# Six of ten gate and value projections of a hybrid decoder block go from seven half-size products to plain products, and the rest are spread one half-step to two other jobs

## The chip, the core and the metric

The kernel runs on one core of a Trainium2 chip. TensorE (PE) multiplies matrices into PSUM, VectorE (DVE) and ScalarE (ACT) work elementwise, GpSimd (POOL) and SyncE (SP) issue DMAs here. The metric is the device time of one execution in microseconds.

## The reference

One layer on 256 tokens of width 2048, all in float32. `h` is the normalised input; one wide projection of it feeds four branches, each is gated, projected back and merged through sigmoid gates that are projections of `h` too; then an output projection, a residual and a last norm.

```python
h = rmsnorm(x, norm_g)
proj = jnp.einsum('bsd,df->bsf', h, w_in)            # 2048 -> 18432, split in 14 pieces
ya = stick_breaking_attention(a_q, a_k, a_v) * jax.nn.silu(a_g)
yb = conformer_conv(b_a, b_b, ...) * jax.nn.silu(b_g)
yc = spatial_gating(jax.nn.gelu(c_u), jax.nn.gelu(c_v), ...) * jax.nn.silu(c_g)
yd = dilated_mixture(d_q, d_k, d_v) * jax.nn.silu(d_g)
yproj = jnp.einsum('bsnc,ncd->bsnd', branches, w_branch)
gates = jax.nn.sigmoid(jnp.einsum('bsd,df->bsf', h, w_gate) + b_gate)
merged = jnp.sum(gates * yproj, axis=2)
return x + jnp.einsum('bsd,de->bse', merged, w_out)  # then rmsnorm(x, final_g)
```

## The kernel before

Every weight is read once or twice from HBM as a tile of 128 x 2048 (1 MB) and split into a high part `hi` (a rounded copy, ScalarE, line 87) and a low part `lo` (the difference, VectorE, line 88). Three products, high by high, low by high and high by low, give nearly float32 precision. `xhl` holds the two parts of the normalised input, `xuh` and `xul` those of the input before the division by its norm.

The work is a list `prog` of jobs. `run` walks it: at position t it issues the loads of job t+5, the split of job t+2, the addition of job t+4, then the matmuls of job t, what follows them (`post`), and whatever `later` has put at this position. Each engine takes its instructions in that order. Kinds of job:

- T (`proj_t`, lines 254 and 257): one weight tile as the stationary side, 16 matmuls of 512 columns and 16 of 256 into one bank of the pool `ps_t`; ScalarE and VectorE empty it (lines 286, 287). 120 of them.
- N (`mm_n`, lines 307 to 309): a weight tile as the moving side, 24 matmuls of 512 columns into a pair of banks. Two make a block of 512 columns of a branch's projection, four one of the other projections.
- H (`group`, line 429): a group of 256 x 2048 by 2048 x 1024 is done by seven products of half-size blocks instead of eight (Strassen's scheme in Winograd's form). Each product is two halves H of 12 matmuls. Factors of the weights are sums of tiles, made in place by `do_add` (line 120, VectorE), those of the input are made once by `make_sx`; the products are combined out of PSUM (lines 408 and 412). A group is 14 H. A gate group adds its bias by one matmul with a constant.

There are ten groups: two for each of the four branches' gates, and the values `a_v` and `c_v`. They stand in a `queue`, from which `step` mixes them in among T and N. Eight N of the values `d_v` come first, on `xuh` and `xul`, scaled afterwards, while the normalisation runs on VectorE. Then follow the convolution's projections, the dilated attention's heads (`d_head`; the convolution's taps and norm on VectorE beside them), the b gates, branch d, the attention pairs (`a_pair`), branches b and a, the c units and branch c, and the output projection. Loaded tiles turn in a ring of six (`st`); gates and values go to DRAM and come back (`gl`, `v`).

## Time and profile before

| what | value |
|---|---|
| time, median of 2 runs (range) | 1641.81 us (1639.13 to 1644.49) |
| the profiled execution: own time, span | 1643.87 us, 1642.2 us |
| TensorE matmuls busy | 1475.0 us, 90% |
| VectorE busy | 1262.8 us, 77% |
| ScalarE busy | 862.5 us, 53% |
| mean granted clock of TensorE | 0.963 |
| DMA | 391.87 MB, mean 239 GB/s |

A busy line gives an engine's time in instructions; PEld is the loading of stationary operands, which overlaps the matmuls. In the view by windows each row is a stretch of the span in microseconds: its length, each engine's busy time with the number of instructions, TensorE's granted clock as a share of full speed, the share of the time that the DMA engines move data, and their rate. In the view by groups a row is a line of the kernel, engine and operation: count, busy time, mean length in ns, and the idle time ahead of them with what ended it. In the view of waits a row is who waited for whom: time in total, number, longest.

### The profile page before, as it was taken

The page shows a single profiled execution, that of the slowest core. Times are in us where ns is not written, and L with a number is a line of the kernel's source. Part 1 is how long each engine was busy: PE and PEld are TensorE (multiplying, and loading weights), DVE is VectorE, ACT ScalarE, POOL GpSimd, SP SyncE. Part 2 cuts the span into 40 slices and gives each one's busy share as a digit, 9 for nine tenths or more (in the row PEclk, how much of TensorE's full clock was granted, in tenths as well). Part 3 has the DMA queues.
Part 4 walks back from the last instruction along what each step waited for, and adds up shares of the span by engine and source line. Part 5 has one row for each costly group of instructions (what it writes and reads, how often), then busy time and mean ns, then how long its engine had stood idle before and what let it go on. Part 6 is the DMA issues. An engine that isn't in the chain of part 4 may idle for free. (4 is left out here: it accounts for less than half of the span.)

```text
span 1642.2 us, 18166 instructions
## 1 busy us (share of the span) xinstructions
PE 1475.0 (90%) x7204; PEld 1227.0 (75%) x7204; DVE 1262.8 (77%) x1232; ACT 862.5 (53%) x773; POOL 86.9 (5%) x160
## 2 busy tenths in 40 slices
PE   7889999999966979999997989878989979978997
PEld 6778888888855767777786877766867768856786
DVE  7588888888778878988776766768778587897654
ACT  6344444444445555754566575656544367755342
POOL 0100000000000000011000000000111200001000
PEclk9999999999998989999999999998999999999999
DMA  8555545554417758799874845756988766869551
GB/s 340 206 186 180 186 173 193 180 181 169 163 52 260 287 200 320 264 336 346 280 276 173 316 176 209 258 215 230 348 307 336 316 246 228 316 249 396 192 205 52
DMA packets 65861, 391.87 MB, mean 239 GB/s; under 512 B 8464, under 2 KB 8592, under 8 KB 24688
## 3 DMA queue, kind: packets, MB, share of 16 engines
q1 hardware_dynamic: 47520, 334.66, 54.9%
q0 software_dynamic: 12928, 46.61, 8.1%
q10 hardware_dynamic: 5328, 9.45, 1.6%
q8 instruction: 56, 0.92, 0.2%
q14 instruction: 29, 0.24, 0.0%
HBM read 364.47 MB, written 26.21 MB: 238 GB/s over the span
## 5 line engine op out<-in xcount | busy, mean ns | idle before, releaser
L88 DVE TENSOR_TENSOR lo<-st,hi 128x2048 fp32r<-128x2048 f32 (+2 forms) x318 | 712.7, 2248 | 222.3 <-ACT hi L87 221.7
L254 PE MATMUL ps<-xhl,hi 128*128 128x512 f32 x1920 | 698.2, 405 | 14.4 <-DVE dst L287 11.5
L87 ACT ACTIVATE hi<-st 128x2048 fp32r<-128x2048 f32 (+2 forms) x318 | 594.6, 1877 | 187.2 <-DVE st L120 64.8
L257 PE MATMUL ps<-xhl,lo 128*128 128x256 f32 x1920 | 526.2, 284 | 19.0 <-DVE lo L88 19.0
L254 PEld LDWEIGHTS ps<-xhl,hi 128*128 128x128 f32 x1920 | 365.4, 192 | 94.7 <-DVE dst L287 12.2
L257 PEld LDWEIGHTS ps<-xhl,lo 128*128 128x128 f32 x1920 | 369.4, 192 | 33.5 <-DVE lo L88 24.9
L286 ACT ACTIVATE bt<-ps 128x256 f32<-128x256 f32 x120 | 45.8, 382 | 319.9 <-PE ps L254 319.9
L120 DVE TENSOR_TENSOR st<-st 128x2048 f32<-128x2048 f32 x80 | 182.8, 2286 | 18.9 <-DMA st<-in_w_dram 18.6
L637 DVE SCALAR_TENSOR_TENSOR cv<-glu,vec_sb,cv 128x255 f32<-128x255 f32 (+14 forms) x240 | 112.2, 468 | 6.6
L429 PE MATMUL X<-hi,xhl 128*128 128x512 f32 x320 | 108.9, 407 | 6.7 <-DVE p L412 6.6
L429 PE MATMUL X<-hi,s 128*128 128x512 f32 x320 | 108.2, 404 | 6.3 <-ACT hi L87 6.3
L307 PE MATMUL psy<-hi,yh 128*128 128x512 f32 x256 | 102.2, 399 | 9.1 <-DVE gl L577 7.2
L308 PE MATMUL psy<-lo,yh 128*128 128x512 f32 x256 | 102.3, 400 | 6.9 <-DVE lo L88 6.9
L309 PE MATMUL psy<-hi,yl 128*128 128x512 f32 x256 | 101.3, 396 | 0.0
L287 DVE TENSOR_TENSOR dst<-ps,bt 128x256 f32<-128x256 f32 x120 | 50.4, 420 | 48.9 <-ACT bt L286 48.6
L429 PEld LDWEIGHTS X<-hi,xhl 128*128 128x128 f32 x320 | 63.1, 197 | 21.7 <-ACT hi L87 6.1
L429 PEld LDWEIGHTS X<-hi,s 128*128 128x128 f32 x320 | 62.3, 195 | 19.7 <-ACT hi L87 7.2
L429 PE MATMUL X<-lo,s 128*128 128x512 f32 x160 | 65.4, 409 | 11.3 <-DVE lo L88 11.2
L429 PE MATMUL X<-lo,xhl 128*128 128x512 f32 x160 | 65.4, 409 | 6.4 <-DVE lo L88 6.4
L307 PEld LDWEIGHTS psy<-hi,yh 128*128 128x128 f32 x256 | 48.9, 191 | 22.5 <-ACT hi L87 5.7
L308 PEld LDWEIGHTS psy<-lo,yh 128*128 128x128 f32 x256 | 49.1, 192 | 19.4 <-DVE lo L88 9.6
L429 PE MATMUL Y<-hi,xhl 128*128 128x512 f32 x160 | 54.5, 406 | 5.7 <-ACT hi L87 5.7
(249 smaller groups left out, 1528.3 us busy)
## 6 DMA issues: line engine op xcount, KB each, us to landing
st<-in_w_dram SPq DMA_DIRECT2D x314, 1024.0 KB, 5.6
gl<-g_dr POOLq DMA_DIRECT2D x32, 256.0 KB, 7.8
m_dr<-gl POOLq DMA_DIRECT2D x24, 256.0 KB, 6.6
ml<-m_dr POOLq DMA_DIRECT2D x24, 256.0 KB, 6.7
g_dr<-p ACTq DMA_DIRECT2D x16, 256.0 KB, 6.6
g_dr<-u ACTq DMA_DIRECT2D x8, 256.0 KB, 6.6
g_dr<-g ACTq DMA_DIRECT2D x8, 256.0 KB, 4.8
xr<-in_x_dram POOLq DMA_DIRECT2D x8, 256.0 KB, 4.4
```

Of the source, the lines that this page charges most:

```text
L87: A.activation(hi, src, AF.Copy)
L88: V.tensor_sub(lo, src, hi.bitcast(F32))
L120: V.tensor_add(self.st[:], self.st[:], self.other[:])
L254: T.matmul(ps[:], hi[:, o:o + P], rhs[:, k, :], start=start, stop=stop)
L257: T.matmul(ps[:, 0:S], lo[:, o:o + P], rhs[:, k, 0:S], start=False, stop=False)
L286: A.activation(bt[:], ps[:, S:2 * S], AF.Copy)
L287: V.tensor_add(dst[:, j, :], ps[:, 0:S], bt[:])
L307: T.matmul(ps[tb][:], lh(k0 + kk, 0, tb), hi[:, o:o + 512], start=st, stop=False)
L308: T.matmul(ps[tb][:], lh(k0 + kk, 0, tb), lo[:, o:o + 512], start=False, stop=False)
L309: T.matmul(ps[tb][:], lh(k0 + kk, 1, tb), hi[:, o:o + 512], start=False, stop=sp)
L429: T.matmul(ps[:], lh(k, part), w_[:, o:o + 512], start=fresh and kk == i == 0, stop=j == 1 and kk == 3 and i == 2, skip_group_check=not first)
L637: V.scalar_tensor_tensor(dst, src, wc, dst, op0=ALU.mult, op1=ALU.add)
```

## The change

Four parts.

1. Of ten groups four stay seven products (gates of b and a). The gates of d and c become plain N jobs (`gate_plain`: four N for each 512 columns), and so do the values a_v and c_v (`v_plain`). `gate_plain` adds its bias by VectorE from a broadcast row (`bgb`), out of PSUM, and applies the sigmoid one job later.
2. `a_v` moves to the start, behind `d_v`, on the unnormalised `xuh` and `xul`; eight more N stand ahead of the first T. The normalisation's pieces move to later jobs, one to a job. The gate bias of the groups left is loaded two jobs ahead of its use.
3. `put` takes one H from the queue for every second main job, from the dilated attention's last head to the c gates. `later` counts sizes, with H as 0.5. Branch a moves behind the c gates. `when` holds the attention's scores back until the pair before is done.
4. The split is issued in two: the high part ahead of the addition, the low part behind it. The tiles of the fourth block of weights (B tiles) are loaded again where they are used again, not kept.

```diff
-        def do_split(self):
+        def do_hi(self):
+            if self.split is None:
+                self.hl = new_hi()[:], new_lo()[:]
+                A.activation(self.hl[0], self.st[:], AF.Copy)
+
+        def do_lo(self):
             if self.split is not None:
-                self.hl = self.split(self.st)
-            else:
-                self.hl = new_hi()[:], new_lo()[:]
-                split(*self.hl, self.st[:])
+                if not self.cut:
+                    self.hl = self.split(self.st)
+            elif not self.cut:
+                V.tensor_sub(self.hl[1], self.st[:], self.hl[0].bitcast(F32))
+            self.cut = True
...
     def later(n, fn):
-        calls.setdefault(now[0] + n, []).append(fn)
+        t, left = now[0], n
+        while left > 0 and t + 1 < len(prog):
+            t += 1
+            left -= prog[t].size
+        calls.setdefault(max(t, now[0] + 1), []).append(fn)
...
+    def put(job):
+        prog.append(job)
+        mains[0] += 1
+        if mains[0] % 2 == 0:
+            step()
...
-            for k, (ahead, name) in enumerate(((LOAD_AHEAD, "do_load"), (SPLIT_AHEAD, "do_split"), (ADD_AHEAD, "do_add"))):
+        stages = ((LOAD_AHEAD, "do_load"), (SPLIT_AHEAD, "do_hi"), (ADD_AHEAD, "do_add"), (SPLIT_AHEAD, "do_lo"))
...
-        p7 = [half("X", "s3", j, tile_of(1, 0, j), plus=(lambda: bs[0]) if j == 0 else tile_of(1, 1, 1),
-                   keep=hold_other(bs, 1) if j else None,
-                   post=(lambda: done(1, 1, V_.tensor_sub, "p5", "X", "p5")) if j else None) for j in range(2)]
-        p3[1].src, p3[1].keep = (lambda: bs[1]), None
-        jobs += [p3[0], p7[0], p7[1], p3[1]]
+        p7 = [half("X", "s3", j, tile_of(1, 0, j), plus=tile_of(1, 1, j),
+                   post=lambda: done(1, 1, V_.tensor_sub, "p5", "X", "p5")) for j in range(2)]
...
+        return p1 + p2 + p5 + p6 + p3 + p7 + p4
...
+    def gate_plain(b, c):
+        bi, acc = BRANCH[b], {}
+        def fetch():
+            acc["b"] = sm2_p.tile([P, 512], F32, tag="ml", name="bgb")
+            o = c * 512
+            nc.gpsimd.dma_start(acc["b"][:], bgb[bi, :, o:o + 512].to_broadcast([P, 512]))
+        def mm(q):
+            def fn(hi, lo):
+                if q == 0:
+                    acc["ps"] = n_banks(1, "psg")
+                mm_n(acc["ps"], (hi, lo), 4 * q, x_lh, q == 0, q == 3)
+            return fn
+        def out_g():
+            for tb in range(2):
+                g = so_p.tile([P, 512], F32, tag="so", name="g")
+                V.tensor_add(g[:], acc["ps"][tb][:], acc["b"][:])
+                later(1, lambda tb=tb, g=g: out_s(tb, g))
+        def out_s(tb, g):
+            A.activation(g[:], g[:], AF.Sigmoid)
+            nc.scalar.dma_start(g_dr[bi, tb, :, c * 512:(c + 1) * 512], g[:])
+            stored.add((b, c, tb))
+        for q in range(4):
+            put(Job(("gateN", bi * 4 + c, q), mm(q), keep=(lambda st: fetch()) if q == 0 else None,
+                    post=out_g if q == 3 else None))
...
+    d_out = v_plain("d_v", AF.Copy, xu_lh, (xu_banks(ps_n, "n"), xu_banks(ps_x, "x")), True, first_job)
+    a_out = v_plain("a_v", AF.Copy, xu_lh, (xu_banks(ps_t, "t"), xu_banks(ps_n, "n")), True)
+    at = {0: lambda: nc.sync.dma_start(cst_sb[:], cst[:, 0:C_K]), 3: h_squares, 5: lambda: (h_rms(), h_split(0)),
+          6: lambda: h_split(1), 7: lambda: h_split(2), 8: lambda: h_split(3), 9: h_rstd,
+          10: lambda: d_out(0), 11: lambda: d_out(1), 12: lambda: a_out(0), 13: gate_bias_load,
+          15: lambda: later(1, lambda: (a_out(1), gate_bias()))}
...
         if h0 == 6:
-            queue += gate_group("d", 0) + gate_group("d", 1) + v_group("a_v", None)
-        d_head(h0 + 1, pair, 6 if h0 == 6 else 0)
+            for b in "ba":
+                queue += gate_group(b, 0) + gate_group(b, 1)
+        d_head(h0 + 1, pair)
...
+    for c in range(4):
+        gate_plain("d", c)
     for i in range(0, 8, 2):
         b_gate(i)
-    step(len(queue))
-    for b in "ba":
-        queue += gate_group(b, 0) + gate_group(b, 1)
-    step(2)
-    branch("d", first=True, n=1)
+    branch("d", first=True)
...
-    queue += v_group("c_v", AF.Gelu_apprx_tanh) + gate_group("c", 0) + gate_group("c", 1)
-    branch("b", n=1)
-    branch("a", n=1)
+    v_plain("c_v", AF.Gelu_apprx_tanh)
+    branch("b")
...
     for i in range(8):
-        c_unit(i, 1 if i < 6 else 2)
+        c_unit(i)
+    for c in range(4):
+        gate_plain("c", c)
     step(len(queue))
+    branch("a")
```

What VectorE's queue holds around the first attention pair's softplus before, from the second scores (line 828) to the first sum (854); `lo` is the low part of a later job's weights, `st` a sum of two tiles, `pr_a` the low part that the sums on TensorE need:

```order
L828 SCALAR_TENSOR_TENSOR ph_a_5912<-z_6366,ph_a_5912 128x384
L88 TENSOR_TENSOR lo_6376<-st_5979,hi_6375 128x2048
L120 TENSOR_TENSOR st_6047<-st_6047,st_6346 128x2048
L287 TENSOR_TENSOR dst_6380<-ps_6381,bt_6414 128x256
L837 SCALAR_TENSOR_TENSOR ph_a_5912<-ph_a_5912 128x768
L88 TENSOR_TENSOR lo_6422<-st_6299,hi_6421 128x2048
L842 TENSOR_TENSOR pr_a_5913<-ph_a_5912,pr_a_5913 128x768
L88 TENSOR_TENSOR lo_6444<-st_6047,hi_6443 128x2048
L854 TENSOR_TENSOR ph_a_5912<-ph_a_5912,cc_6459 128x384
```

The same stretch of the changed kernel, where the lines are 881, 891, 896 and 908 and the split's low part is line 134:

```order
L881 SCALAR_TENSOR_TENSOR ph_a_6041<-z_6410,ph_a_6041 128x384
L134 TENSOR_TENSOR lo_6420<-st_6305,hi_6419 128x2048
L314 TENSOR_TENSOR dst_6373<-ps_6423,bt_6456 128x256
L891 SCALAR_TENSOR_TENSOR ph_a_6041<-ph_a_6041 128x768
L134 TENSOR_TENSOR lo_6467<-st_6347,hi_6466 128x2048
L134 TENSOR_TENSOR lo_6487<-st_6367,hi_6486 128x2048
L314 TENSOR_TENSOR dst_6490<-ps_6491,bt_6524 128x256
L896 TENSOR_TENSOR pr_a_6042<-ph_a_6041,pr_a_6042 128x768
L122 TENSOR_TENSOR st_6482<-st_6482,st_6484 128x2048
L134 TENSOR_TENSOR lo_6532<-st_6417,hi_6531 128x2048
L314 TENSOR_TENSOR dst_6490<-ps_6536,bt_6569 128x256
L908 TENSOR_TENSOR ph_a_6041<-ph_a_6041,cc_6572 128x384
```

From softplus to the low part there was one split of an H between, now two splits and a T's eviction; from there to the sum one split before, now an addition, a split and an eviction.

VectorE's queue where the first group's products begin to alternate with T before (line 710 is the dilated attention's output, 412 a combination of two products):

```order
L88 TENSOR_TENSOR lo_3983<-st_3844,hi_3982 128x2048
L120 TENSOR_TENSOR st_3673<-st_3673,st_3948 128x2048
L88 TENSOR_TENSOR lo_4009<-st_3892,hi_4008 128x2048
L120 TENSOR_TENSOR st_3724<-st_3724,st_3980 128x2048
L710 TENSOR_TENSOR dst_3468<-o_4026,dst_3468 128x256
L88 TENSOR_TENSOR lo_4033<-st_3673,hi_4032 128x2048
L287 TENSOR_TENSOR dst_3898<-ps_4036,bt_4069 128x256
L88 TENSOR_TENSOR lo_4075<-st_3724,hi_4074 128x2048
L120 TENSOR_TENSOR st_3673<-st_3673,st_4030 128x2048
L412 TENSOR_TENSOR p1_3999<-Y_4013,p1_3999 128x512
```

The changed kernel at the same place, in the d gates (line 539 takes a gate block out of PSUM and adds its bias, 762 is the dilated attention's output):

```order
L539 TENSOR_TENSOR g_4677<-psg_4515,bgb_4334 128x512
L539 TENSOR_TENSOR g_4679<-psg_4516,bgb_4334 128x512
L762 TENSOR_TENSOR dst_3724<-o_4681,dst_3724 128x256
L134 TENSOR_TENSOR lo_4689<-st_4590,hi_4688 128x2048
L134 TENSOR_TENSOR lo_4709<-st_4148,hi_4708 128x2048
L122 TENSOR_TENSOR st_3980<-st_3980,st_4706 128x2048
L134 TENSOR_TENSOR lo_4747<-st_4646,hi_4746 128x2048
L134 TENSOR_TENSOR lo_4778<-st_4686,hi_4777 128x2048
L134 TENSOR_TENSOR lo_4798<-st_3980,hi_4797 128x2048
L122 TENSOR_TENSOR st_4148<-st_4148,st_4795 128x2048
```

Additions stood behind every split or every second one; now one stands to three splits, with the two bias additions per block between.

More of the change, by code (lines that the diff above doesn't have):

```diff
@@ L413, in done, with half @@
             sink(tb, c, box[t], op is not None)
-        def half(acc, name, j, src, plus=None, first=False, post=None, keep=None):
+        def half(acc, name, j, src, plus=None, first=False, post=None, keep=None, prev=None):
             def mm(hi, lo):
@@ L430, in mm @@
                                  stop=j == 1 and kk == 3 and i == 2, skip_group_check=not first)
-            return Job(src, mm, plus=plus, post=post, keep=keep)
-        def hold(d, j):
-            return lambda st, other: d.__setitem__(j, st)
-        def hold_other(d, j):
-            return lambda st, other: d.__setitem__(j, other)
-        V_ = V
-        jobs = [half("X", "a11", j, tile_of(0, 0, j), first=True, keep=hold(ts, j),
-                     post=(lambda: keep(("X", "p1"))) if j else None) for j in range(2)]
@@ L443, in group @@
-        jobs += [half("Y", "a12", j, tile_of(0, 1, j), first=True,
-                      post=(lambda: done(0, 0, V_.tensor_add, "Y", "p1", "p1")) if j else None) for j in range(2)]
-        jobs += [half("Z", "s1", j, lambda j=j: ts[j], plus=tile_of(1, 0, j), first=True,
-                      post=(lambda: keep(("Z", "p5"))) if j else None) for j in range(2)]
-        jobs += [half("X", "s2", j, lambda j=j: ts[j], plus=tile_of(1, 1, j),
-                      post=(lambda: keep(("X", "u2"))) if j else None) for j in range(2)]
@@ L455, in group, with held @@
-        jobs += [p3[0], p7[0], p7[1], p3[1]]
-        jobs += [half("X", "a22", j, lambda j=j: ts[j], plus=tile_of(0, 1, j),
-                      post=(lambda: done(1, 0, None, "X", "X", "X")) if j else None) for j in range(2)]
-        return jobs
+            return Job(src, mm, plus=plus, post=post if j else None, keep=keep, prev=prev, size=0.5)
+        def held(j):
+            return lambda: ts[j]
+        V_ = V
+        p1 = [half("X", "a11", j, tile_of(0, 0, j), first=True, keep=lambda st, j=j: ts.__setitem__(j, st),
+                   post=lambda: keep(("X", "p1"))) for j in range(2)]
@@ new lines, in group @@
+        p2 = [half("Y", "a12", j, tile_of(0, 1, j), first=True,
+                   post=lambda: done(0, 0, V_.tensor_add, "Y", "p1", "p1")) for j in range(2)]
+        p5 = [half("Z", "s1", j, held(j), plus=tile_of(1, 0, j), first=True, prev=p1[j],
+                   post=lambda: keep(("Z", "p5"))) for j in range(2)]
+        p6 = [half("X", "s2", j, held(j), plus=tile_of(1, 1, j), prev=p5[j],
+                   post=lambda: keep(("X", "u2"))) for j in range(2)]
+        p3 = [half("Z", "n4", j, tile_of(1, 1, j),
+                   post=lambda: done(0, 1, V_.tensor_sub, "Z", "u2", "u2")) for j in range(2)]
@@ new lines, in v_plain, with mm, fn, out_v @@
+    def v_plain(name, func, lh=None, pairs=None, scale=None, jobs=None):
+        acc = {}
+        def mm(c, q):
+            def fn(hi, lo):
+                if q == 0:
+                    acc[c] = pairs[c]() if pairs else n_banks(1, "psv")
+                mm_n(acc[c], (hi, lo), 4 * q, lh or x_lh, q == 0, q == 3)
+            return fn
+        def out_v(c):
+            for tb in range(2):
+                t = so_p.tile([P, 512], F32, tag="so", name="v")
+                A.activation(t[:], acc[c][tb][:], func, scale=rstd_n[:, tb:tb + 1] if scale else 1.0)
+                nc.gpsimd.dma_start(v_dr[name][:, tb, c * 512:(c + 1) * 512], t[:])
+                stored.add((name, c, tb))
+        for c in range(2):
+            for q in range(4):
+                e = ("inN", OFF[name] // 512 + c, q)
+                if jobs is not None and c == 0:
+                    prog.append(jobs(q, e, mm(c, q)))
+                else:
+                    put(Job(e, mm(c, q), post=(lambda c=c: out_v(c)) if q == 3 and not scale else None))
+        return out_v
@@ L542, in job_y, with branch @@
         return job
-    def branch(b, first=False, sink=None, n=0):
+    def branch(b, first=False, sink=None):
         bi = BRANCH[b]
@@ L921, in hybrid_block, with c_unit @@
     marker(c_begin)
-    def c_unit(i, n):
+    def c_unit(i):
         def mix(ug):
```

119 lines of the change are left out of this document (50 added, 69 removed).

## The prediction

> **What bounds the kernel now.** I read the page's totals first, then the busy time by stage, with the stages cut where the kind of TensorE work changes.
>
> ```profile
> span 1642.2 us, 18166 instructions
> PE 1475.0 (90%) x7204; PEld 1227.0 (75%) x7204; DVE 1262.8 (77%) x1232; ACT 862.5 (53%) x773; POOL 86.9 (5%) x160
> ```
>
> ```profile
> core 0: us, PE busy (x) PEld busy (x) DVE busy (x) ACT busy (x) POOL busy (x), PEclk, DMA share, GB/s
> 0.00:106.90 106.90, 86.36 (x393) 70.77 (x394) 77.03 (x94) 54.64 (x64) 5.47 (x14) 0.94 0.67 252
> 106.90:445.80 338.90, 338.81 (x1944) 295.76 (x1943) 283.76 (x487) 152.72 (x167) 3.87 (x6) 1.00 0.51 182
> 445.80:505.85 60.05, 35.24 (x168) 28.62 (x167) 43.54 (x53) 27.37 (x33) 0.56 (x1) 0.85 0.19 74
> 505.85:729.40 223.55, 201.37 (x949) 164.96 (x948) 193.45 (x129) 133.26 (x107) 8.98 (x17) 0.96 0.75 282
> 729.40:801.40 72.00, 68.13 (x291) 55.14 (x289) 53.85 (x31) 34.52 (x22) 8.49 (x17) 0.98 0.90 319
> 801.40:1118.05 316.65, 274.98 (x1331) 229.57 (x1330) 226.69 (x147) 193.29 (x165) 4.92 (x8) 0.94 0.63 229
> 1118.05:1146.10 28.05, 24.75 (x93) 19.62 (x93) 24.02 (x16) 17.83 (x13) 2.14 (x4) 0.86 0.76 284
> 1146.10:1291.60 145.50, 136.00 (x578) 109.41 (x578) 114.07 (x77) 66.87 (x42) 27.52 (x52) 0.98 0.88 331
> 1291.60:1430.00 138.40, 126.28 (x673) 107.18 (x672) 103.17 (x90) 88.19 (x83) 12.06 (x20) 0.98 0.70 265
> 1430.00:1491.80 61.80, 46.87 (x189) 35.03 (x188) 58.49 (x35) 37.92 (x28) 3.76 (x7) 0.97 0.78 294
> 1491.80:1543.60 51.80, 47.58 (x216) 38.15 (x215) 34.48 (x30) 19.11 (x15) 6.96 (x13) 1.00 0.83 315
> 1543.60:1642.20 98.60, 88.63 (x395) 72.77 (x393) 50.25 (x53) 36.77 (x39) 2.15 (x4) 0.98 0.38 134
> ```
>
> From 106.9 to 445.8 TensorE never rests; from 1430.0 to 1491.8 VectorE is busy 58.49 of 61.80 and TensorE has holes. So the bound changes by stage, and a sum needs a price per job. Three kinds of job fill TensorE: T (one 128-column tile of weights for a transposed projection, 32 matmuls), N (a plain step, 24 matmuls of 512 columns) and H (half of one of the seven products, 12 such matmuls). Two ScalarE rows that each close a T job, fourteen jobs apart, and two TensorE rows 24 matmuls apart give the prices when nothing waits:
>
> ```profile
> 112.74 0.38 ACT L286 ACTIVATE bt<-ps 128x256 f32<-128x256 f32 x1 [3.41 <-PE ps L254]
> 191.88 0.38 ACT L286 ACTIVATE bt<-ps 128x256 f32<-128x256 f32 x1 [3.40 <-PE ps L254]
> ```
>
> ```profile
> 18.10 0.39 PE L307 MATMUL psv<-hi,xuh 128*128 128x512 f32 x1
> 23.54 0.39 PE L307 MATMUL psv<-hi,xuh 128*128 128x512 f32 x1
> ```
>
> T is 79.14/14 = 5.65 us, N 5.44, H half of N, 2.72. The program has 120 T, 56 N and 140 H: 678.0 + 304.6 + 380.8 = 1363.4 us. The other 279 us are waits, slow clock and small matmuls. By stage (length less its jobs), from the top: 23.8, 22.5, 32.1, 35.9, 1.1, 80.6, 9.0, 14.9, 18.1, 21.0, 8.3, 11.6. That list is what the change can work on; the 80.6 (attention pairs with H at three per two T) and the 35.9 (three H per T) are its largest.
>
> **The change part by part.** *Products.* Six groups go from 14 H to 8 N: 8 x 5.44 - 14 x 2.72 = 5.44 us more each, 32.7 us in all, and eight bias matmuls (0.23 us each, a 24th of N) leave with four gate groups, 1.8 us. TensorE gets 30.9 us more work. This is certain and on the path wherever TensorE doesn't wait.
>
> *VectorE and ScalarE.* The group rows price what goes:
>
> ```profile
> L88 DVE TENSOR_TENSOR lo<-st,hi 128x2048 fp32r<-128x2048 f32 x308 | 702.7, 2288 | 220.9 <-ACT hi L87 220.3
> L120 DVE TENSOR_TENSOR st<-st 128x2048 f32<-128x2048 f32 x80 | 182.8, 2286 | 18.9 <-DMA st<-in_w_dram 18.6
> L412 DVE TENSOR_TENSOR p<-Y,p 128x512 f32<-128x512 f32 x10 | 6.8, 682 | 0.0
> L577 DVE TENSOR_TENSOR gl<-psy,gl 128x512 f32<-128x512 f32 x32 | 21.7, 685 | 6.7 <-PE psy L309 6.6
> L87 ACT ACTIVATE hi<-st 128x2048 fp32r<-128x2048 f32 x308 | 586.0, 1909 | 185.6 <-DVE st L120 64.8 <-PE psy L309 63.3 <-PE pso L309 11.6
> ```
>
> Gone are 36 splits (82.4 us), 48 tile additions (109.7) and 18 combinations (12.3); new are 16 bias additions out of PSUM, not in this trace, taken as L577's 0.685 (a read of PSUM and one of SBUF): 11.0. VectorE falls by 193 us to about 1070, ScalarE by 36 x 1.909 = 69 at least. At two mains per H VectorE needs, per 14.0 us of two T and one H, three splits 6.9, 0.57 additions 1.3 and the evictions: under 10.
>
> *Spacing.* Groups now take one H per two mains. The trace holds a stretch with exactly that mix, the later c units:
>
> ```profile
> 1340.60:1430.00 89.40, 89.40 (x488) 77.04 (x487) 68.69 (x58) 63.17 (x60) 6.59 (x11) 1.00 0.72 267
> ```
>
> TensorE has no hole in 89.40 us there, VectorE is busy 77%, the loads move at 267 GB/s. I carry this to every stage that gets the mix, and take away what its waits cost. The longest of them, and the chain behind the largest:
>
> ```profile
> PE cc L851 <- DVE pr_a L842: 16.2, 4, 4.5
> PE pp L699 <- ACT p L408: 13.5, 1, 13.5
> DVE st L120 <- DMA st<-in_w_dram: 18.6, 13, 2.8
> PE ps L254 <- DVE dst L287: 11.5, 2, 6.5
> ```
>
> ```profile
> 867.75 0.55 DVE L828 SCALAR_TENSOR_TENSOR ph_a<-z,ph_a 128x384 f32<-128x384 f32 x1
> 872.64 0.85 ACT L832 ACTIVATE ph_a<-ph_a 128x768 f32<-128x768 f32 x1
> 880.06 0.95 DVE L837 SCALAR_TENSOR_TENSOR ph_a<-ph_a 128x768 f32<-128x768 f32 x1
> 885.93 0.95 DVE L842 TENSOR_TENSOR pr_a<-ph_a,pr_a 128x768 fp32r<-128x768 f32 x1
> 886.93 0.47 PE L851 MATMUL cc<-pr_a 128*128 128x128 f32 x1 [4.49 <-DVE pr_a L842]
> ```
>
> From the scores to the sums the chain takes 19 us, and splits and additions stand between its links. Before, two T and two or three H lay between (14 us at their price); now, with `later` counting sizes, three T and an H (19.7), with less in the queues. I leave 8 of the attention stages' non-small waits; with about 13 of small matmuls (102 of them, at a little over half of N's 5.44/24 = 0.227, an estimate) 80.6 + 9.0 becomes 21. The 35.9 becomes 10 (small 3.5, the rest for bank handovers in the four new d gates); the 21.0, all H before, lies now in the c gates: 3. The 32.1 is the conv norm's chain and the making of the factors, which stays: there a T and an H more now stand ahead of the transposes that waited 13.5, 8.4 us of cover, so 23.6.
>
> *Start.* Eight more N run on unnormalised x ahead of the first T, and the normalisation's quarters are spread one to a job.
>
> ```profile
> 45.03 1.67 DVE L234 SCALAR_TENSOR_TENSOR xt<-xt,vec_sb,rstd 128x256 f32<-128x256 f32 x4
> 47.83 1.23 DVE L88 TENSOR_TENSOR xhl<-xt,xhl 128x1024 fp32r<-128x1024 f32 x1 [1.13 <-ACT xhl L87]
> 82.59 0.69 DVE L475 TENSOR_TENSOR b<-b,b 128x512 f32<-128x512 f32 x1 [10.60 <-DMA b<-in_bg_dram]
> 1311.78 1.29 DVE L907 BATCH_NORM_STATS2 bst<-vc 128x6 f32<-128x512 f32 x2 [8.21 <-DMA vc<-v_dr_c_v]
> ```
>
> A quarter (1.67 + 1.13 + 1.23) and a split are 6.3 us of VectorE in an N of 5.44, so four quarters fall about 4 behind; the 10.60 behind the gate bias goes, since its loads are issued two jobs earlier. 23.8 - 10.6 + 4 = 17. If the loads came late all the same, 27.
>
> *c norm.* Its tile is still fetched after the preceding branch frees its space, and VectorE again waits for it (8.21, with all splits queued behind): 18.1 becomes 16; if it landed in time, 6.
>
> *Branches and handovers.* Plain groups and branches d, b, a take turns on one pair of banks. An H covers 2.72 us at each handover but in branch a, which now runs bare.
>
> ```profile
> L307 PE MATMUL psy<-hi,yh 128*128 128x512 f32 x256 | 102.2, 399 | 9.1 <-DVE gl L577 7.2 <-DVE ml L965 1.9
> ```
>
> Twelve such handovers cost 7.2 together, 0.6 each; bare ones about 1.3 (two evictions of 0.685). Branch d 1.1 becomes 3, branches b and a 14.9 becomes 8.
>
> *B tiles reread*: two more loads in each of the four groups, 8 in all, against 36 fewer in the other six; taken at 0, since the loads run ahead in their ring of tiles. Without that cover it is the last rival below.
>
> Sum: jobs 1363.4 + 32.7 = 1396.1; rest 17 + 22.5 + 23.6 + 10 + 3 + 21 + 8 + 16 + 3 + 19.9 (the last two as before) = 144. Together 1540 against the span's 1642.2. The profiled run's own 1643.87 is 1.7 above its span and 2.1 above the median, 1641.81, so 1540 is also the forecast.
>
> By the Trainium skill (Perfetto Trace Analysis, Identifying the Most-Contended Engine) headroom on TensorE is judged by the share of weight loading, not of matmuls. That is 75%, which would leave room for 415 us. The stretch without a hole shows 77.04 of 89.40, 86%: here TensorE is full well below 100% of it, and I keep my prices.
>
> By the Trainium skill (TensorE: Matmul & The Clock Gate, The HAM clock gate) an idle window of about 3.4 us halves the clock until as long a busy one. The granted clock of 0.85 in the conv norm's stage and 1.00 in the one before it agree: part of each removed wait comes back as clock, already inside the rests above.
>
> **The rivals.** *Latency stays.* The attention chains are long in themselves (two ScalarE table changes, four crossings between engines), so if their own length and not the queues made the 80.6, it stays: the two attention stages then give their last 9.0 and not 68.6, and of the 102 won 43 are left: 1600. Against: the cover grows from 14 to 19.7. Chance 0.08.
>
> *Handover.* Each of the 22 groups on one pair waits for a split in hand (2.29) and two to four evictions (1.4 to 2.7) less the H's 2.72: 1 to 2.3 each, 5 in bare branch a: 40 to 60 more, 1590. For: the 6.5 of the row for `ps`; against: 0.6 each so far. Chance 0.06. By the Trainium skill (Perfetto Trace Analysis, Optimizing Tensor Performance) independent groups should rotate through different banks so that one's eviction lies beside the next one's matmuls, which these do not; the 0.6 each is what this trace shows of it.
>
> *The ring of loads, slower.* Two of six tiles are now held over 11 H and 22 mains, and an addition's second tile is loaded one step before it. A tile lands late:
>
> ```profile
> st<-in_w_dram SPq DMA_DIRECT2D x314, 1024.0 KB, 5.6
> ```
>
> If each of the 32 additions waits for a slot (a split, 2.29) and a landing (5.6), 7.9 us, VectorE stands 253 us, 60 more than it saved, with every split and eviction behind: 1642 + 31 and up to 60, 1700. It decides from 193/32 = 6.0 us each. Against: 18.6 over 80 additions, and no hole in the stretch with this mix. Chance 0.04.
>
> That the change doesn't do what it says is out: the order of instructions has 272 full splits and 32 additions.
>
> **How the numbers follow.** Forecast 0.76 (1508 to 1580: low if c norm's tile lands in time, -10, factors hide better, -10, and attention and gates leave nothing, -12; high if the attention stages, gates, handovers and start keep twice what I left them, +40), latency 0.08, handover 0.06, ring 0.04, and 0.06 for under 1508, more overlap than I see. The range 1508 to 1592 holds the forecast and half of handover, some 0.8. Two per cent, 33 us, is about what this measurement tells from no change: below 1609 is faster, which takes in all but the slower part of latency (0.05) and the ring: 0.91; within 0.05; slower 0.04.
>
> **What would show it.** Right: TensorE near full from the d gates to the c gates, granted clock 0.99 there, VectorE near 1070, `cc` and `pp` gone from the longest waits, first T near 105. Wrong: additions waiting for loads over 2 us each, holes at each first matmul on the plain pair, or attention pairs above 1.2 of their jobs' price.

## The result and the profile after

The changed kernel takes 1587.17 us (median of 1586.43 and 1587.91) against 1641.81 before: a ratio of 0.967, 95% interval 0.960 to 0.974. It is faster, by 54.6 us of the 102 that were forecast, and inside the range of 1508 to 1592, 5 us below its upper end. The question of this study is where the other 47 us went.

The totals of the changed kernel's page, and two of its groups on VectorE, the low parts of the splits (L134) and the additions (L122):

```profile
span 1583.4 us, 18279 instructions
PE 1487.2 (94%) x7340; PEld 1246.4 (79%) x7340; DVE 1080.6 (68%) x1146; ACT 776.1 (49%) x712; POOL 91.6 (6%) x168
...
L134 DVE TENSOR_TENSOR lo<-st,hi 128x2048 fp32r<-128x2048 f32 x272 | 621.2, 2292 | 249.0 <-ACT hi L127 248.9
...
L122 DVE TENSOR_TENSOR st<-st 128x2048 f32<-128x2048 f32 x32 | 73.2, 2288 | 76.7 <-DMA st<-in_w_dram 76.7
```

The work is what the prediction priced: 272 splits, 32 additions, VectorE at 1080.6 (forecast 1070), ScalarE down by 86.4. One row is not: 32 additions wait 76.7 us for loads, 2.4 us each, where 80 of them waited 18.6 before. That is one of the three signs which the prediction gave for being wrong. (The attention, the third of them, lies at 1.16 times its jobs' price, below the 1.2 named.)

The busy time by stage, cut at the first job of each; the rows shown are the last dilated heads with the d and b gates, the attention with c_v, branch b, the c units and the c gates.

```profile
core 0: us, PE busy (x) PEld busy (x) DVE busy (x) ACT busy (x) POOL busy (x), PEclk, DMA share, GB/s
...
545.41:739.77 194.36, 186.75 (x893) 156.09 (x891) 122.60 (x91) 100.30 (x85) 8.25 (x15) 0.99 0.73 264
...
802.43:1060.03 257.60, 244.77 (x1251) 206.37 (x1250) 161.08 (x116) 149.66 (x135) 8.14 (x14) 0.98 0.62 227
1060.03:1123.68 63.65, 56.80 (x241) 46.21 (x241) 40.06 (x30) 26.98 (x16) 12.15 (x23) 0.95 0.83 298
1123.68:1256.69 133.01, 120.83 (x636) 102.78 (x635) 92.93 (x85) 81.81 (x79) 12.34 (x20) 0.96 0.71 259
1256.69:1378.47 121.78, 116.24 (x502) 95.38 (x501) 80.60 (x48) 60.15 (x42) 5.92 (x11) 0.97 0.76 281
```

With the prediction's prices (T 5.65, N 5.44, H 2.72) each stage has a rest, which is its length less the price of its jobs. The first of these rows holds 10 T, 16 N and 14 H, 181.6 us, so its rest is 12.7. Attention holds 24 T, 8 N and 16 H, 222.6 us, rest 35.0. All the rests, beside two experiments that are told below:

| stage | forecast | changed | e1: additions three ahead | e9: held, split first |
|---|---|---|---|---|
| start | 17 | 17.2 | 17.0 | 19.0 |
| first T stage and conv norm | 46.1 | 42.9 | 43.0 | 42.8 |
| d and b gates | 10 | 12.7 | 4.1 | 5.4 |
| branch d | 3 | 8.3 | 2.5 | 2.5 |
| attention with c_v | 21 | 35.0 | 24.3 | 32.8 |
| branches b and a | 8 | 16.7 | 9.1 | 15.7 |
| c units | 16 | 20.9 | 17.5 | 14.9 |
| c gates | 3 | 10.3 | 0.9 | 2.5 |
| branch c and out | 19.9 | 23.4 | 23.4 | 23.0 |
| sum | 144 | 187.3 | 141.7 | 158.6 |

The jobs, 1396.1, and the rests, 187.3, make the span of 1583.4. Of the 47 us, 43 are rests above the forecast and 4 lie between the span and the median. Everything up to the conv norm came about as forecast. The overrun begins where the groups begin.

A group's seven products are p1 to p7, each in two halves, and p5, p6, p7 and p4 need an addition in each half; p7 is the one whose halves load both tiles of their sum. Here is VectorE's timeline of the changed kernel around the first half of p7 in the first of the four groups, and the SyncE issue that matters there:

```profile
645.85 2.29 DVE L134 TENSOR_TENSOR lo<-st,hi 128x2048 fp32r<-128x2048 f32 x1 [1.26 <-ACT hi L127]
648.58 2.29 DVE L134 TENSOR_TENSOR lo<-st,hi 128x2048 fp32r<-128x2048 f32 x1 [0.43 <-ACT hi L127]
658.41 2.29 DVE L122 TENSOR_TENSOR st<-st 128x2048 f32<-128x2048 f32 x1 [7.54 <-DMA st<-in_w_dram]
660.62 4.49 DVE L134 TENSOR_TENSOR lo<-st,hi 128x2048 fp32r<-128x2048 f32 x2
```

```profile
650.90 0.33 SPq L99 DMA_DIRECT2D st<-in_w_dram  x1
```

The split's low part (L134) ends at 650.87 and frees a tile of the ring. At 650.90 the load of the addition's second tile starts in it. The addition (L122) is the very next instruction on VectorE, so VectorE stands for the whole landing, 7.54 us, and the low parts of the two jobs that TensorE needs next stand behind it. Waits of this kind stand at seven of the eight halves of p7. The exception is the second half in the third group (1123.93), which comes up behind other work and doesn't wait; the first half of the product after it, p4, waits there instead (1144.88). In the second group a link of the attention's chain stands between the split and the addition. The other rows:

```profile
675.43 2.29 DVE L122 TENSOR_TENSOR st<-st 128x2048 f32<-128x2048 f32 x1 [7.53 <-DMA st<-in_w_dram]
880.34 2.29 DVE L122 TENSOR_TENSOR st<-st 128x2048 f32<-128x2048 f32 x1 [5.39 <-DMA st<-in_w_dram]
899.53 2.29 DVE L122 TENSOR_TENSOR st<-st 128x2048 f32<-128x2048 f32 x1 [4.55 <-DMA st<-in_w_dram]
1102.94 2.29 DVE L122 TENSOR_TENSOR st<-st 128x2048 f32<-128x2048 f32 x1 [9.10 <-DMA st<-in_w_dram]
1123.93 2.29 DVE L122 TENSOR_TENSOR st<-st 128x2048 f32<-128x2048 f32 x1
1144.88 2.29 DVE L122 TENSOR_TENSOR st<-st 128x2048 f32<-128x2048 f32 x1 [7.60 <-DMA st<-in_w_dram]
1325.03 2.29 DVE L122 TENSOR_TENSOR st<-st 128x2048 f32<-128x2048 f32 x1 [8.59 <-DMA st<-in_w_dram]
1341.58 2.29 DVE L122 TENSOR_TENSOR st<-st 128x2048 f32<-128x2048 f32 x1 [7.06 <-DMA st<-in_w_dram]
```

Together these eight waits are 57.4 of the 76.7 us, the seven of p7 alone 49.8. What they cost TensorE shows best behind the longest one. The eviction of a pair of banks (`gl`, L647) stands behind that addition on VectorE, and TensorE can't start its next sum in the pair before it:

```profile
1108.18 0.77 PE L333 MATMUL psy<-hi,yh 128*128 128x512 f32 x1 [5.02 <-DVE gl L647]
```

The theory put to the test: these additions hold VectorE up because p7 fills the ring of six (two tiles held by the group, two for the half, two for the jobs between, counted from the program), and two parts of the change make that matter, the reread of the B tiles and the low part's new place behind the addition. The rivals: DMA is too slow in itself, or the handover of the plain groups' banks makes the holes. The kernel before took 1644.51, 1643.40, 1644.84 and 1643.92 us beside the four sets of runs below (e1 to e4, e5 to e8, e9 to e11, e12); each ratio is against its own. The changed kernel's 1587.17 was taken beside the 1641.81, and times below are compared with it as they stand.

### The profile page after: what moved, and what is told of

It reads as the page before. It is cut to its first block, busy times and chain, and to the rows that moved or that the text cites. A ratio compares the mean times of both kernels' runs of the same rounds, so it can differ in the third digit from the quotient of the medians.

```text
span 1583.4 us, 18279 instructions
## 1 busy us (share of the span) xinstructions
PE 1487.2 (94%) x7340; PEld 1246.4 (79%) x7340; DVE 1080.6 (68%) x1146; ACT 776.1 (49%) x712; POOL 91.6 (6%) x168
## 4 chain that ended last, share of the span: by engine, by line
PE 35%; DVE 6%; DMA 6%; ACT 4%; issue 3%; POOL 0%; DVEq 0%; ACTq 0%; POOLq 0%
PE ps L281 6%; DVE lo L134 3%; PE ps L284 3%; PE psy L334 3%; PE X L458 3%; PE psy L333 3%; DMA st<-in_w_dram 3%; PE psy L335 3%; ACT hi L127 2%; PE pso L334 2%; PE pso L335 2%; PE pso L333 2%; PE psg L334 2%; PE psg L333 2%; PE psg L335 2%
## 5 line engine op out<-in xcount | busy, mean ns | idle before, releaser
L134 DVE TENSOR_TENSOR lo<-st,hi 128x2048 fp32r<-128x2048 f32 x272 | 621.2, 2292 | 249.0 <-ACT hi L127 248.9
L281 PE MATMUL ps<-xhl,hi 128*128 128x512 f32 x1920 | 697.5, 406 | 14.9 <-ACT hi L127 5.8
L127 ACT ACTIVATE hi<-st 128x2048 fp32r<-128x2048 f32 x272 | 517.0, 1910 | 249.8 <-PE psy L335 95.3
L284 PE MATMUL ps<-xhl,lo 128*128 128x256 f32 x1920 | 526.9, 285 | 25.9 <-DVE lo L134 25.8
L122 DVE TENSOR_TENSOR st<-st 128x2048 f32<-128x2048 f32 x32 | 73.2, 2288 | 76.7 <-DMA st<-in_w_dram 76.7
L334 PE MATMUL psg<-lo,xhl 128*128 128x512 f32 x256 | 101.1, 395 | 6.1 <-DVE lo L134 6.1
L333 PE MATMUL psg<-hi,xhl 128*128 128x512 f32 x256 | 101.4, 396 | 1.9 <-ACT hi L127 1.9
L335 PE MATMUL psg<-hi,xhl 128*128 128x512 f32 x256 | 100.9, 394 | 0.0
L314 DVE TENSOR_TENSOR dst<-ps,bt 128x256 f32<-128x256 f32 x120 | 50.6, 421 | 72.9 <-ACT bt L313 72.6
L333 PEld LDWEIGHTS psy<-hi,yh 128*128 128x128 f32 x256 | 49.8, 194 | 30.8 <-ACT hi L127 13.7
L334 PEld LDWEIGHTS psg<-lo,xhl 128*128 128x128 f32 x256 | 48.9, 191 | 17.1 <-DVE lo L134 7.0
L333 PEld LDWEIGHTS psg<-hi,xhl 128*128 128x128 f32 x256 | 48.8, 191 | 12.6 <-issue 2.3
L335 PEld LDWEIGHTS psy<-hi,yl 128*128 128x128 f32 x256 | 49.9, 195 | 10.7
L333 PE MATMUL psv<-hi,xuh 128*128 128x512 f32 x128 | 51.6, 403 | 7.0 <-ACT hi L87 7.0
```

What stands on the lines that cost most here:

```text
L122: V.tensor_add(self.st[:], self.st[:], self.other[:])
L127: A.activation(self.hl[0], self.st[:], AF.Copy)
L134: V.tensor_sub(self.hl[1], self.st[:], self.hl[0].bitcast(F32))
L281: T.matmul(ps[:], hi[:, o:o + P], rhs[:, k, :], start=start, stop=stop)
L284: T.matmul(ps[:, 0:S], lo[:, o:o + P], rhs[:, k, 0:S], start=False, stop=False)
L314: V.tensor_add(dst[:, j, :], ps[:, 0:S], bt[:])
```

## The experiments

**e1, additions three jobs ahead.** One number is changed.

```diff
-ADD_AHEAD = 4
+ADD_AHEAD = 3
```

> An addition is queued on VectorE three jobs ahead instead of four. Ring theory: at four jobs ahead a half of p7 needs all six tiles of the ring at once (two held, its own two, those of the two jobs between), so its second load starts only when the split just ahead of it on VectorE ends, and VectorE stands for a landing: 57.4 of the 76.7 us that the additions wait, in eight of them. Three ahead, one tile is spare: the eight waits fall from 7.2 to under 2 us each, the additions' wait in all to under 25, and about 20 to 30 us of span go (TensorE's excess at the p7 halves was 31). Rival (DMA itself too slow or the plain groups' handover makes these holes): the waits move to the next instruction and the time stays within 8 us of 1587.

1540.10 us, ratio 0.9365 (0.9349 to 0.9381): 47 us faster than the changed kernel, more than either theory expected. The additions' group, and VectorE around the same half of p7:

```profile
L122 DVE TENSOR_TENSOR st<-st 128x2048 f32<-128x2048 f32 x32 | 73.1, 2285 | 10.8 <-DMA st<-in_w_dram 10.8
```

```profile
648.36 2.29 DVE L134 TENSOR_TENSOR lo<-st,hi 128x2048 fp32r<-128x2048 f32 x1 [0.43 <-ACT hi L127]
653.79 2.29 DVE L134 TENSOR_TENSOR lo<-st,hi 128x2048 fp32r<-128x2048 f32 x1 [3.14 <-ACT hi L127]
658.28 2.29 DVE L122 TENSOR_TENSOR st<-st 128x2048 f32<-128x2048 f32 x1 [2.20 <-DMA st<-in_w_dram]
```

The additions' wait falls from 76.7 to 10.8. But the reason given in the expectation, one tile more to spare, is wrong for this half: the addition starts at 658.28, about as before (658.41), since its load lands no earlier. What is new is the split at 653.79 in between, which used to stand behind the addition. The order of SyncE's loads, of TensorE's and of ScalarE's work is the same in both programs, and so is VectorE's but for the place of the 32 additions; a few transfers on GpSimd's queue differ too. So the 47 us are not the landing but what waited behind the waiting instruction. Stage by stage:

```profile
545.20:730.94 185.74, 184.73 (x892) 154.93 (x890) 122.59 (x91) 100.41 (x85) 8.25 (x15) 1.00 0.77 276
...
787.85:1034.76 246.91, 240.17 (x1251) 203.28 (x1250) 159.28 (x115) 150.01 (x135) 8.15 (x14) 1.00 0.65 235
1034.76:1091.33 56.57, 54.74 (x242) 45.09 (x241) 42.52 (x31) 27.14 (x16) 12.15 (x23) 1.00 0.93 336
1091.33:1220.96 129.63, 119.66 (x635) 102.22 (x634) 90.77 (x85) 81.93 (x79) 13.26 (x20) 0.95 0.72 267
1220.96:1333.39 112.43, 112.43 (x502) 93.24 (x500) 83.14 (x49) 60.19 (x42) 5.91 (x11) 1.00 0.83 306
```

TensorE has no hole left in the c gates (112.43 of 112.43) and 1 us in 185.74 of the d and b gates, at a granted clock of 1.00 where it was 0.97 and 0.99. The loads move at 306 and 276 GB/s there, more than before the edit, so DMA was not the limit, and no bank was touched, so the handover rival falls too: TensorE's waits for `gl`, 9.3 us in the changed kernel, are 1.5 here.

**e3, the low part ahead of the addition.** The stages of a step in the order of the kernel before, additions still four ahead.

```diff
-(ADD_AHEAD, "do_add"), (SPLIT_AHEAD, "do_lo"))
+(SPLIT_AHEAD, "do_lo"), (ADD_AHEAD, "do_add"))
```

> In each step VectorE's second half of a split is queued ahead of the addition and not behind it, as in the kernel before; additions stay four jobs ahead, B tiles are reread. Ring theory: the split of job t+2 frees its tile ahead of the addition for t+4, so that one tile of six is spare, as with additions three ahead: the eight waits fall to 0 to 3 us each, the additions' wait to under 30, and 15 to 30 us of span go. Rival: no change within 8 us, since the load would still land at the same time.

1567.73 us, ratio 0.9531 (0.9517 to 0.9545): 19 us faster, as the ring theory expected, with 25.8 us of waits left. VectorE at the two halves of p7 in the second group:

```profile
867.92 2.29 DVE L122 TENSOR_TENSOR st<-st 128x2048 f32<-128x2048 f32 x1 [3.00 <-DMA st<-in_w_dram]
870.13 0.42 DVE L314 TENSOR_TENSOR dst<-ps,bt 128x256 f32<-128x256 f32 x1
870.46 1.01 DVE L908 TENSOR_TENSOR ph_a<-ph_a,cc 128x384 f32<-128x384 f32 x2
...
887.37 2.29 DVE L122 TENSOR_TENSOR st<-st 128x2048 f32<-128x2048 f32 x1 [4.55 <-DMA st<-in_w_dram]
889.58 0.42 DVE L314 TENSOR_TENSOR dst<-ps,bt 128x256 f32<-128x256 f32 x1
889.91 0.55 DVE L881 SCALAR_TENSOR_TENSOR ph_a<-z,ph_a 128x384 f32<-128x384 f32 x1
```

Here no split stands behind the addition, but an eviction (L314) and a link of the attention's chain (L908, L881) do. In e1 the addition comes behind the finished job's evictions and chain links. The order of the loads, of TensorE's work and of splits and additions among themselves is the same in e1 and e3, so that place is worth 27.6 us. Attention keeps a rest of 33.3 in e3 and 24.3 in e1.

**e2, B tiles held.** The reread is undone, with the order of the kernel before. Of the edit, the line that sets the order:

```diff
-        return p1 + p2 + p5 + p6 + p3 + p7 + p4
+        return p1 + p2 + p5 + p6 + [p3[0], p7[0], p7[1], p3[1]] + p4
```

(p7's first half adds p3's first tile, p3's second half takes p7's second, as before.)

> The B tiles are held instead of reread, in the order p3, p7, p7, p3 of the kernel before; everything else as in the changed kernel; 8 loads fewer. Ring theory: the first half of p7 adds a tile that has landed long ago and waits for nothing; the second half still loads two tiles with two held, so its wait stays. The additions' wait falls from 76.7 to about 45 and the time by 10 to 18 us. If the reread alone were the cause, all of the 57 us of waits go and 25 to 35 us of time. If the loads' count or their bytes made it, no more than 8 x 2.5 us of DMA time spread over the run, under 5 us.

1573.77 us, ratio 0.9569 (0.9553 to 0.9586): 13 us faster, as the ring theory expected of one half. The two halves of p7 in the first group, the second half in the third group, and the additions as a group:

```profile
639.72 2.29 DVE L123 TENSOR_TENSOR st<-st 128x2048 f32<-128x2048 f32 x1 [1.76 <-DMA st<-in_w_dram]
...
658.55 2.29 DVE L123 TENSOR_TENSOR st<-st 128x2048 f32<-128x2048 f32 x1 [7.42 <-DMA st<-in_w_dram]
...
1100.54 2.29 DVE L123 TENSOR_TENSOR st<-st 128x2048 f32<-128x2048 f32 x1 [9.32 <-DMA st<-in_w_dram]
```

```profile
L123 DVE TENSOR_TENSOR st<-st 128x2048 f32<-128x2048 f32 x32 | 73.2, 2288 | 59.3 <-DMA st<-in_w_dram 59.2
```

The half with a held tile waits 1.76, the one that loads two tiles 7.42. The sum fell less than expected (59.3, not 45). Over the four groups the first halves wait 5.1 us in place of 30.6, but the second ones 31.1 in place of 19.1, above all in the third group, where the wait of 9.32 is new.

**e9, both undone.** B tiles held and the low part first, the two edits of e2 and e3 together.

> Both parts of the change that take the spare tile are undone together: B tiles held, and the split queued ahead of the addition; additions stay four ahead, the two-to-one spacing and all else stay. Alone they won 13 and 19 us. Ring theory: with both, no half of p7 asks for more than five tiles at once, and of the additions' 76.7 us of waits under 15 stay: 1542 to 1558. If the two only move the wait between each other: no better than the better of them, 1562 to 1570.

1559.81 us, ratio 0.9479 (0.9463 to 0.9495), 27 us faster than the changed kernel and 2 us above the range expected. The additions' wait is 15.7:

```profile
L123 DVE TENSOR_TENSOR st<-st 128x2048 f32<-128x2048 f32 x32 | 73.2, 2286 | 15.7 <-DMA st<-in_w_dram 15.7
```

So 27 of the 47 us belong to these two parts of the change, somewhat less than the sum of 13 and 19. Some 20 more (1560 to 1540) the forecast took for granted, and undoing the two parts doesn't give them: the table shows most of them in attention (32.8 against 24.3) and branches b and a (15.7 against 9.1). What makes them is the place of the additions ahead of evictions, as the next run shows.

**e10, additions three ahead and B tiles held.**

> Additions three ahead, and the B tiles held instead of reread. Ring theory: the spare tile is there already, so holding wins nothing and the 8 rereads cost nothing: within 6 us of 1540. If the rereads cost something of their own (8 loads of 1 MB, some 2.6 us each), up to 20 us faster.

1545.06 us, ratio 0.9391 (0.9379 to 0.9404), 5 us behind e1. Once the additions stand in the right place, the 8 rereads cost nothing, as the prediction took them; holding costs a little, in attention (rest 27.5 against 24.3). From e9 this run differs on VectorE only in the place of the additions: the splits and additions have the same order among themselves, and so have all other instructions, but the additions come behind the evictions. That is 14.8 us faster (1559.81 to 1545.06), a second price for the place, with the tiles held.

**e5, the kernel before with additions three ahead.** The same number, in the other program.

> The kernel before with additions three jobs ahead and nothing else changed. Ring theory: in the kernel before splits were queued ahead of additions and B tiles held, so a tile was spare and its 80 additions waited 18.6 us in all; there is little to win: 1632 to 1648, and the 47 us that the same edit won in the changed kernel (1587 to 1540) belong to what the change did to the ring. Rival (three ahead is simply better for any order of this program): 20 us or more faster, below 1622.

1715.81 us, ratio 1.0444 (1.0416 to 1.0473): 72 us slower. No theory had that. Its additions wait for no load at all; ScalarE waits for them. First ScalarE's waits for additions in the kernel before, then in this run (us in total, times, the longest), then ScalarE and VectorE of this run in a stretch where halves stand side by side:

```profile
ACT hi L87 <- DVE st L120: 64.8, 29, 5.8
```

```profile
ACT hi L87 <- DVE st L120: 280.2, 69, 7.3
```

```profile
529.47 1.92 ACT L87 ACTIVATE hi<-st 128x2048 fp32r<-128x2048 f32 x1 [4.22 <-DVE st L120]
...
535.95 1.91 ACT L87 ACTIVATE hi<-st 128x2048 fp32r<-128x2048 f32 x1 [4.08 <-DVE st L120]
```

```profile
527.09 2.28 DVE L120 TENSOR_TENSOR st<-st 128x2048 f32<-128x2048 f32 x1
531.42 2.29 DVE L88 TENSOR_TENSOR lo<-st,hi 128x2048 fp32r<-128x2048 f32 x1 [2.04 <-ACT hi L87]
533.63 2.29 DVE L120 TENSOR_TENSOR st<-st 128x2048 f32<-128x2048 f32 x1
537.89 2.29 DVE L88 TENSOR_TENSOR lo<-st,hi 128x2048 fp32r<-128x2048 f32 x1 [1.98 <-ACT hi L87]
```

Whole splits are queued ahead of additions in that program, so three ahead puts each addition directly in front of its own split: addition 2.28, high part 1.92, low part 2.29, one after the other, 6.5 us from one addition to the next (527.09 to 533.63), for a half that TensorE does in 2.72. In the changed kernel two things are different: the low part of another job stands between an addition and its own split, and two whole jobs stand between two halves. The next run keeps only the second of them.

**e12, additions three ahead and the low part first.** The edits of e1 and e3 together.

> The changed kernel with additions three ahead and the low part of the split ahead of the addition: each addition then stands directly in front of its own split, as in the kernel before with three ahead, but with two whole jobs to one half. If halves that adjoin made that kernel 72 us slower (6.5 us in series for 2.72 us of TensorE), the spacing covers it here: 6.5 us for the half, two splits of 2.29 and 1.4 to 2.7 of evictions are 12.5 to 13.8 of 13.6 us, so 1540 to 1560. If the place of the low part is what makes three ahead work, ScalarE's wait for additions comes back at each of 32 additions with 2 to 4 us: 1580 and above.

1561.78 us, ratio 0.9499 (0.9483 to 0.9514), 22 us slower than e1 and 2 us above the range expected of the spacing. ScalarE's wait for additions in e12 and in e1:

```profile
ACT hi L127 <- DVE st L122: 149.3, 31, 7.0
```

```profile
ACT hi L127 <- DVE st L122: 42.2, 20, 5.3
```

So both theories hold in part. ScalarE's wait does come back, 4.8 us at nearly each of the 32 additions, but with two whole jobs to a half it costs 22 us in all, not 72. Four ahead with the low part first (e3) and three ahead with it behind (e1) are the same order of splits and additions; e12 is one place further, and already too late, since its own split is the next. The additions in e12 wait for no load at all, and yet it is slower than e1.

**e6, the reread alone.** The kernel before, with B tiles reread in its ten groups, 20 loads more.

```diff
-        jobs += [p3[0], p7[0], p7[1], p3[1]]
+        jobs += p3 + p7
```

> The kernel before with the B tiles reread in all ten groups (20 more loads, order p3 p3 p7 p7) and nothing else: this part of the change alone. If one spare tile of the ring is what matters, the cost is that of the DMA alone: halves stand side by side there, and 20 loads at about 2.6 us (1 MB at some 400 GB/s) are at most 52 us, part of it hidden: 1645 to 1680. If the reread costs a wait of 7 us in each half of p7 wherever it stands, as in the changed kernel: 20 x 7 = 140 us of VectorE waits, at least 80 us slower, above 1720. If loads are hidden as the prediction took them: within 5 us of 1644.

1699.44 us, ratio 1.0343 (1.0313 to 1.0372), 56 us slower (2.8 us for each added load), 19 us above the range for DMA time alone and well below the 80 of a full wait at each half.

```profile
L120 DVE TENSOR_TENSOR st<-st 128x2048 f32<-128x2048 f32 x80 | 182.9, 2287 | 44.0 <-DMA st<-in_w_dram 41.0
```

The additions wait 25 us more than before (18.9), half of the loss; whether the other half is the loads' own time among adjoining halves or what waited behind the additions, this run does not tell. It does show that a reread has no fixed price: 2.8 us each here, and in e1, which rereads, nothing that holding them (e10) would win.

**e4, delays counted in jobs.** In the changed kernel a half counts 1 again.

```diff
-            return Job(src, mm, plus=plus, post=post if j else None, keep=keep, prev=prev, size=0.5)
+            return Job(src, mm, plus=plus, post=post if j else None, keep=keep, prev=prev, size=1.0)
```

> Delays are counted in jobs again: a half product counts 1 and not 0.5, so the links of the attention chains lie 14.0 us of jobs apart (two T and one H) in place of up to 19.7. Cover theory (the prediction's): the chain of about 19 us comes out from under its cover, the matmuls of the sums and of the values wait 3 to 5 us in each of four pairs, and some in the d heads and gates: 10 to 30 us slower than the changed kernel, 1597 to 1617. Queue theory (the spacing alone won it, the count does nothing): within 8 us of 1587.

1602.62 us, ratio 0.9746 (0.9727 to 0.9766), 15 us slower than the changed kernel, inside the range of the cover theory. The wait that the prediction followed through its chain, for the second part of softplus ahead of the sums, is back:

```profile
PE cc L905 <- DVE pr_a L896: 14.9, 4, 4.2
```

Before it was 16.2 in four waits; in the changed kernel TensorE does not wait there at all. Attention's rest grows by 10.7 and the conv norm's by 6.1 (in the profiled execution, at 1607.07 the longest of the four).

**e7, e8 and e11, what is left.** All three have additions three ahead. e7 writes the fetch of c norm's tile ahead of the four setup loads of the c branch; e8 also gives branch a two pairs of banks in turn (`n_banks(c if sink or b == "a" else 1, "psy")`); e11 is e8 without e7's edit, with the tile fetched on SyncE's queue:

```diff
-        nc.gpsimd.dma_start(vc[:], v_dr["c_v"][:])
+        nc.sync.dma_start(vc[:], v_dr["c_v"][:])
```

> Additions three ahead, and in front of the c units the tile of c norm is fetched ahead of the four setup loads (2 MB) on GpSimd's queue instead of behind them. With additions three ahead alone that tile took 14.7 us to land and VectorE waited 5.3 us for it, weight loads beside it took 10 to 11.6 us. If the order of that queue is the cause: the tile lands in under 9 us, VectorE's wait is under 1 us, the rest of the c units falls from 17.5 to 8 to 12 us, 1531 to 1536 in all. If the slot that the tile waits for is the cause (it started when a split freed it), the rest stays above 15 us and the time at 1540.

> As the run before it, and branch a takes its accumulators from two pairs of banks in turn, as branch c does. Handover rival: the rest of branch a, 6.9 us with additions three ahead, falls to 2 to 4 us (its three bare handovers go). If its rest is the last wait for the split of branch c's input (3.7 us at its end), only about 1 to 3 us go. Either way between 0 and 5 us faster than the run before it.

> Additions three ahead, branch a on two pairs of banks in turn, and c norm's tile fetched by SyncE's queue, whose order is the written one (on GpSimd's the rewritten order changed nothing, that tile still went last). If the four setup loads ahead of it in the queue delay it: it lands in under 10 us, VectorE's 5 us wait for it goes, and the c units' rest falls from 16.6 to 9 to 12: 1530 to 1534. If it waits for its slot, or lands no earlier beside the setup loads: within 3 us of 1538.

e7: 1543.21 us (1539.19 to 1547.55), ratio 0.9386 (0.9349 to 0.9422), no change. In its trace GpSimd fetches the tile last all the same, so the run doesn't test its question. e8: 1537.93 us, 0.9357 (0.9334 to 0.9380); branch a's rest falls from 6.9 to 3.7, so about half of it was handover, and the 3.57 us that TensorE waits at its end for ScalarE's `hi` stay. The total moves too little to tell it from e1. e11: 1536.63 us, 0.9340 (0.9325 to 0.9355), the lowest, though not told apart from e8; the c units' rest is 13.1 against 16.6 in e8. VectorE's wait for the tile in e1 and in e11:

```profile
DVE bst L958 <- DMA vc<-v_dr_c_v: 5.3, 1, 5.3
```

```profile
DVE bst L958 <- DMA vc<-v_dr_c_v: 2.4, 1, 2.4
```

The tile lands 9.7 us after its issue in place of 14.7, and half of the wait stays. The time is within the 3 us of 1538 that were expected if the queue is not the cause, so what holds the tile up stays open. e11 beats the changed kernel by 51 us and the kernel before by 108.

## Why the prediction was right or wrong

*The number* lies inside the range, but for a reason that the range did not have. Its upper end was meant for stages that keep twice the rest they were left; gates, branches and attention did keep between 1.7 and 2.3 times theirs, because of the additions' waits. That the two come to much the same is luck. Of the signs for being right, the loads of VectorE, `cc` and `pp` and the first T came; TensorE near full at a granted clock of 0.99 from the d gates to the c gates did not (0.95 to 0.99 in the rows above).

*The sum of jobs* held: at its prices 1396.1 us of jobs leave 187.3 of the span as rests, and in e1's d and b gates and c gates the jobs' price is met to 4.1 and 0.9 us. VectorE's busy time came 11 us above the forecast, ScalarE's fell by 86.4 where at least 69 were forecast, and the first T came at 104.3 (near 105).

*Start, T stage and conv norm* were right to 3 us (60.1 against 63.1).

*The attention's chain* was right in mechanism: `cc` and `pp` are gone from the longest waits, and e4 brings `cc` back by undoing only the count. That speaks against the rival by which the latency stays. The cover before was misread: "two T and two or three H lay between (14 us at their price)" would be 16.7 at least at the prices given, and in the kernel before's trace one T and two H (11.1) lie between scores and sums in three pairs, and three H (8.2) in the fourth; so the cover, up to 19.7 in the changed kernel, grew by more than was said. The term was mis-sized: 21 forecast, 35.0 measured, 24.3 once the additions are out of the way.

*"B tiles reread ... taken at 0, since the loads run ahead in their ring of tiles"* is the step that failed, together with one that was not costed at all: the low part of the split was moved behind the addition. The loads do not run ahead at p7: the ring is full, the load starts when a split just ahead of the addition ends, and the addition stands there for a landing. The ring rival had this mechanism (7.9 us each) and was nearly right on its price, 7.2 us, but for 8 of 32 additions, not all; and the evidence held against it, the later c units without a hole, came from a program in which the low part stood ahead of the addition and B tiles were held. Undoing both wins back 27 us of the 47; the place of the additions ahead of evictions, which the prediction did not cost either, makes most of the rest (14.8 with tiles held, 27.6 with tiles reread).

*Spacing* ("I carry this to every stage that gets the mix") was right as a possibility and not as an outcome of this order: e1 reaches 4.1 and 0.9 in the gates, better than forecast, and a sum of rests of 141.7 against 144. That the forecast of 1540 is e1's time to the microsecond is partly chance, since branch c with the output, attention and c units are 8.4 above their terms there, and the gates 8.0 below.

*Handover* as a rival is out at 40 to 60 us: e1 closes the holes with the banks untouched, and where a handover was late in the changed kernel, as ahead of 1108.18, an addition held the eviction up. In branch a alone, about 3 us were handover (e8), about 1.1 for each of three bare ones; the forecast had 1.3.

*c norm*: 16 forecast, 20.9 measured, of which e1 takes back 3.4. The wait for its tile, 8.2 us in the kernel before, doesn't show in the changed kernel, where VectorE stands for an addition's load just ahead of it (1144.88); in e1 it is there again, 5.3.

*The two rules of the Trainium skill.* In e1's d and b gates TensorE is almost without a hole (184.73 of 185.74) with weight loading busy 154.93, 83%, so the share of weight loading (Perfetto Trace Analysis, Identifying the Most-Contended Engine) again shows headroom that is not there, and the measurement decides. On the clock gate (TensorE: Matmul & The Clock Gate, The HAM clock gate) the runs are in line with it: in the hole of 5.02 us ahead of 1108.18 the granted clock fell to 0.50 (1105.30 to 1112.00) and was 1.00 again behind it (1112.20 to 1123.68), and over branch b it rose from 0.95 to 1.00 in e1, when the holes closed.

## What to carry to other kernels

An instruction that waits for a load costs what stands behind it on its engine, not its wait: moving 32 additions behind the splits and evictions that were ready won 47 us, though in the half followed above the load landed no sooner. Count the ring at its fullest point, held tiles included, and see which instruction frees the slot that a load needs; if the consumer is queued right behind that one, it waits a whole landing. Of the places tried, one was best: an addition directly behind the split that frees its tile waits for the load (the changed kernel), one directly ahead of its own split makes ScalarE wait (e5, e12), and between the two, behind the evictions, lies e1. A lead counted in jobs has to be set anew when the order within a step or the jobs between change.

## What the runs showed of the hardware

By the Trainium skill (Perfetto Trace Analysis, Optimization Strategy) the same gap repeating on the engine that should be saturated can mean that there is not enough SBUF for the next tile. The eight waits stand on VectorE and reach TensorE as holes (5.02 us ahead of 1108.18), and the ring was full, so the sign fits; but the cure in e1 was an order, with no tile more. A seventh tile was not tried.

GpSimd's one large selection slows VectorE beside it. In e1, GpSimd's timeline and VectorE's:

```profile
1094.31 2.56 POOL L944 TENSOR_SCALAR_AFFINE_SELECT swb<-swb 128x1024 f32<-128x1024 f32 x1 [1.23 <-DMA swb<-in_sgu_wT_dram]
```

```profile
1095.84 5.38 DVE L134 TENSOR_TENSOR lo<-st,hi 128x2048 fp32r<-128x2048 f32 x2
```

Two splits took 5.38 us in place of 4.49 (the row at 660.62 above), and the selection 2.56. In the kernel before the split beside the selection took 2.69 and the selection 1.10. The Trainium skill (GPSIMD Engine Reference, Specifications) has the two engines contend when VectorE's instruction reads two SBUF inputs, as this one does; the rows agree.
